# Hybrid SSD and forgetting-attention layer: where kept-back operand blocks get their high parts, and when three pairs of differences are formed

## The chip, the cores and the metric

The kernel runs on one core of one Trainium2 chip. The time is device microseconds of one execution, from launch to end; lower is better. A core has a matmul engine (TensorE, PE in the profile, with the weight loads shown apart as PEld), a vector engine (DVE), a scalar engine (ACT), a general engine (POOL) and a queue that issues most of the transfers (SP). Each engine works through its own queue of instructions in order and waits at the head of it when an instruction's inputs are not there.

## What is computed

One layer with 1024 positions of 1024 channels, in fp32. A projection makes the inputs of two branches: a chunked Mamba-2 scan, and forgetting attention with 16 heads of 64 channels. The two are gated, projected, merged and projected again.

```
h    = RMSNorm_pre(x);  [z_ssm | xBC | dt | q | k | v | f | z_att | g_ssm | g_att] = h @ w_in
A    = chunked SSD scan of silu(conv(xBC)), normed by groups with silu(z_ssm)
s    = q.k / sqrt(64) + F[t] - F[s],  F = cumsum(log sigmoid(f)),  causal
B    = (softmax(s) @ v) * silu(z_att)
m    = sigmoid(g_ssm) * (A @ w_branch_ssm) + sigmoid(g_att) * (B @ w_branch_att)
out  = x + RMSNorm_post(m @ w_out)
```

## The kernel before

**Seven products for eight.** Every large product (the projection, both branch products, the output product) is cut into 2 by 2 blocks and done with seven block products in place of eight. `Pair` holds one pair of weight columns, `Operands` the seven moving operands of one matrix: four blocks b11, b21, b22 and the differences t1 to t4. The three users in the part that matters are `ops_s` (the scan's output), `ops_a` (the attention's output) and `ops_w` (the output weights). To keep fp32 accuracy each operand is two tiles: a high part, a rounded copy that ScalarE makes, and a low part, the raw value less the high part, which VectorE makes. The operands of one name are four tiles of 128 by 512, j = 0 to 3. In the profile they carry the numbers x0 (b11), x1 (b21), x2 (-b22), x3 (t1), x4 (-t2), x5 (t3) and x6 (t4), with h or l behind. A block product takes twelve matmuls: for each j high by high, high by low, low by high.

**The stream.** `Stream.steps` is a written list of block products. `half()` issues half of one (six matmuls), then lets each `Operands` object under way do a little (`some`), then runs one entry of the list `chores`. `some` counts a step, issues the transfers of up to two raw blocks whose source is there (`fetch`, L257), and makes high and low parts (`split`, L265) of up to two blocks that were fetched more than four steps ago. With a name in `only`, it does whatever that name still lacks; `half()` calls it so just before a product that needs the name.

**The attention loop** has 48 turns, m = 6·hp + g: eight pairs of heads hp, six groups g of query and key blocks. A turn issues, in this order: the score matmuls of the turn, with a VectorE operation each that adds the forget terms and finds the row extreme (L1513), and a ScalarE exponential each (L1517), four of both; the value products of the turn before (`weighted`, tile av); the list `deferred`; `stream.release()`; some halves of the stream ("ahead"); the loads; the transposes of the exponentials (tile pt, in the same four PSUM banks as the scores s) with their copies p to SBUF by ScalarE (L1556) or VectorE (L1554); the outputs of an earlier group (`Heads.out`); then `stream.hold()` and one or two halves more ("behind"). The next turn's score matmuls come after these.

Between `hold()` and `release()` no `some` runs at the end of a half: each is put on the list `held` and run at `release()`, behind the next turn's exponentials. So transfers, high parts and low parts of those halves are kept back until then.

**Differences of the late pairs.** When the attention output of pairs hp = 4 to 7 is done for the second half of the positions (`outputs` with h = 1, called from `out(1)` at the end of the turn with g = 5), the blocks t2 and t3 of j = hp - 4 are formed from it, from t1 (tile x) and from b11 (tile y, loaded at L1577 into one of the four buffers of `small`). The function `second` does this with two VectorE operations (L1602, L1603), and two halves later a chore stores both through POOL's queue (L193). For hp = 4, 5 and 6 `second` goes on the list `deferred` and runs in turn 6·(hp + 1), right after that turn's score operations; `last` (L1617), for t4, runs two turns later and first empties the list of chores.

**What sets the order.** A scheduler orders the instructions of each engine and may move one up when it expects its inputs sooner. `pin` queues an instruction behind the one issued just before it on its engine. Score operations and exponentials are pinned, so are high and low parts and the differences; copies of products (L410), weight parts (L350, L351) and the copies p are not.

Of the kernel before, what the change touches and what calls it, by code (L numbers as in the profile page):

```python
# [11 lines left out]
AF = mybir.ActivationFunctionType  # L12
ALU = mybir.AluOpType
# [73 lines left out]
def hybrid_layer(ctx: ExitStack, tc, a, out):  # L87

    nc = tc.nc
# [43 lines left out]
    def pin(op):  # L133
        return tc.keep_in_program_order(op)
# [7 lines left out]
    second = ExitStack()  # L142
# [16 lines left out]
    class Operands:  # L159
# [9 lines left out]
        def __init__(self, name, src, there=lambda k, h: True, order=lambda op: op, queue=nc.gpsimd):  # L169
            self.src, self.there, self.order, self.queue = src, there, order, queue  # L170
            self.copy = src
            self.tiles, self.left, self.made, self.at, self.step = {}, {}, set(), {}, 0
            self.lows, self.most, self.lag = {}, 1, {}
            self.dram = {n: tc.dram_tile([KH, P, HALF], F32, name=f"{n}_{name}") for n in self.LESS}

        def __getitem__(self, name):
# [85 lines left out]
            r, c = self.BLOCKS.get(block, (0, 0))  # L262
            nc.sync.dma_start(raw, self.copy(KH * r + j, c) if block in self.BLOCKS else self.dram[block][j])

        def split(self, name, j, raw=None):  # L265
            h, l = (t[:, j, :] for t in self.tiles[name])
            if name.strip("-") in self.lows:

                pin(nc.scalar.activation(h, h.bitcast(F32), AF.Copy, scale=-1.0 if name[0] == "-" else 1.0))
                self.left[name].remove(j)  # L270
                return
            if raw is None:
                raw = l.bitcast(F32)
            if name[0] == "-":
                pin(nc.scalar.activation(h, raw, AF.Copy, scale=-1.0))
                pin(nc.vector.scalar_tensor_tensor(l, raw, -1.0, h, ALU.mult, ALU.subtract))
            else:
                pin(nc.scalar.activation(h, raw, AF.Copy))
                pin(nc.vector.tensor_tensor(l, raw, h, ALU.subtract))  # L279
            self.left[name].remove(j)  # L280

        def direct(self, j, y, x):

# [7 lines left out]
                self.at[name, j] = self.step  # L291
                self.split(name, j, raw)

        def some(self, only=None):

            self.step += 1
            n = 0
            for name in list(self.left):
                for j in list(self.left[name]):
                    if (only is None and n < 2 or name == only) and (name, j) not in self.at:  # L300
                        if self.ready(name.strip("-"), j):
                            self.fetch(name, j)
                            self.at[name, j] = self.step
                            n += 1
            n, most = 0, self.most if "merged" in fin else 2
            for name, j in list(self.at):
                if j in self.left[name]:
                    if name == only or only is None and n < most and self.at[name, j] < self.step - 4:
                        self.split(name, j)
                        n += 1  # L310

    def column_halves(key):
# [162 lines left out]
    class Stream:  # L475
# [74 lines left out]
        def half(self):  # L550
# [16 lines left out]
            else:  # L567
# [4 lines left out]
                if p in self.following:  # L572
                    ops = self.following[p]
# [5 lines left out]
            for ops in self.building:  # L579
                if self.held is None:  # L580
                    ops.some()
                else:
                    self.held.append(ops)
            for chores in (self.chores, self.line):
                if chores:
                    chore = chores.pop(0)
                    if chore:
                        chore()
# [11 lines left out]

        def release(self):
            held, self.held = self.held or [], None
            for ops in held:
                ops.some()

# [462 lines left out]
    fin = {}  # L1068
# [113 lines left out]
    with tc.tile_pool(name="pro", bufs=1, reuse_waits="tile", side="right") as pro, tc.tile_pool(  # L1182
        name="prop", bufs=1, space=PSUM, reuse_waits="tile", side="right"
# [7 lines left out]
        low = pro.tile([P, NK, HALF], F32, name="low")  # L1191
# [63 lines left out]
        for j in range(KH):  # L1255
# [11 lines left out]
            with tc.high_priority():  # L1267
# [5 lines left out]
                last = put("-t2", j, t2, -1.0)  # L1273
# [24 lines left out]
    with tc.tile_pool(name="ssm", bufs=1, reuse_waits="tile", side="right") as sp, tc.tile_pool(  # L1298
        name="ssmp", bufs=1, space=PSUM, reuse_waits="tile", side="right"
# [38 lines left out]
    with tc.tile_pool(name="att", bufs=1, reuse_waits="tile", side="right") as ap, tc.tile_pool(  # L1338
# [55 lines left out]
        class Heads:  # L1394
# [16 lines left out]
            def settle(self, n):  # L1411

                if n == 2:
                    return
                nr = ap.tile([P, 2, 2], F32, tag="nr", name="nr")
                dd = self.dd[n] = ap.tile([P, 2, 2, 2], F32, tag="dd", name="dd")
                nm = self.nm[n]
                nc.vector.tensor_tensor(nr, nm[:, :, 0], nm[:, :, 1], ALU.min)
                for h in range(2):
                    nc.vector.tensor_tensor(dd[:, :, h], nr, nm[:, :, h], ALU.subtract)  # L1420
                nc.scalar.activation(dd, dd, AF.Exp)
# [148 lines left out]
                    skip_group_check=True,  # L1570
                )

        state, deferred = {}, []

        def fetched(name, j):
            y = small("y")
# [6 lines left out]
        def outputs(hp, h, zr):  # L1583
# [14 lines left out]
            j, x = hp - KH, state["t"]  # L1598
# [21 lines left out]
            if hp == NK - 1:  # L1620
                second()
            else:

                deferred.append(second if h else last)

        def loads(m):

# [75 lines left out]
        for m in range(6 * NK + 1):  # L1703
# [43 lines left out]
            if m == 6 * NK - 1:  # L1747
                tp = pp.tile([P, HALF], F32, tag="s", bufs=4, name="tp")
                heads[hp].turn(2, tp)
                heads[hp].send(2, tp)  # L1750
            stream.hold()
            stream.halves(behind)
            for hd, which in end(m if m == 6 * NK - 1 else m - 1):
# [60 lines left out]
```

## Time and profile before

| what | time |
|---|---|
| median of 3 runs | 1262.39 us |
| lowest and highest of them | 1260.47 and 1264.7 us |
| the profiled execution, its own time | 1261.39 us |
| its span, first to last instruction | 1259.7 us |
| mean granted TensorE clock of the span | 0.997 |
| attention turns, first to last exponential | 677.4 to 1098.2 us |

The profile is of one execution. Busy times of PE are from modelled ends, so a busy PE may still be held up inside a row of matmuls. Times in the views count from the span's start. In a timeline the bracket behind a row is the idle time of that engine before it and what ended that; rows of one kind that follow each other are merged, with their count. Turn 30, which is spoken of below, has its first exponential at 940.0 us, turn 31 at 950.4 us, turn 47 at 1095.9 us.

### The profile page before, as it was taken

Reading aid. Unit: us, or ns where it says so; the run is one execution under the profiler, and the core shown is the slowest. Engines: PE = TensorE matmul, PEld = TensorE weight load, DVE = VectorE, ACT = ScalarE, POOL = GpSimd, SP = SyncE. Lnnn points to the kernel's source line nnn. Section 1 sums busy time; section 2 is a strip of 40 time slices with the busy share of each in tenths; the row PEclk is TensorE's granted clock in tenths of the full one; section 3 lists DMA queues with packets and bytes.
Section 4 is the critical chain, followed back from the end, with each engine's and each line's share of the span. In section 5 each row is a group of like instructions: output and inputs, shape, how many; then the busy total and the mean of one; then the engine's idle time right before and its main releaser. Section 6 shows DMA issues by size and latency. Waiting matters only on the chain.

```text
span 1259.7 us, 20886 instructions
## 1 busy us (share of the span) xinstructions
PE 1232.9 (98%) x6864; PEld 986.7 (78%) x6864; DVE 1014.3 (81%) x1989; ACT 789.7 (63%) x1735; POOL 336.4 (27%) x384
## 2 busy tenths in 40 slices
PE   5999999999999999999999999999999999999997
PEld 3688888888888888888887777777776777788886
DVE  7998896988788878998766677766789768897975
ACT  7745765556655765567555666666786667843753
POOL 4000440004300241115111333333222232357062
PEclk9999999999999999999999999999999999999999
DMA  8243442646446542744465575666787567756932
GB/s 300 71 124 85 143 155 96 203 149 184 126 128 207 174 134 96 240 145 137 141 213 189 175 260 199 222 208 207 262 301 245 195 207 251 260 201 201 367 118 99
DMA packets 162476, 233.57 MB, mean 185 GB/s; under 512 B 15200, under 2 KB 73024, under 8 KB 162368
## 3 DMA queue, kind: packets, MB, share of 16 engines
q1 hardware_dynamic: 140160, 196.08, 48.7%
q10 hardware_dynamic: 16704, 18.06, 4.0%
q0 software_dynamic: 5504, 18.09, 3.7%
q8 instruction: 54, 0.88, 0.3%
q14 instruction: 54, 0.44, 0.1%
HBM read 162.99 MB, written 72.34 MB: 187 GB/s over the span
## 4 chain that ended last, share of the span: by engine, by line
PE 85%; DVE 5%; DMA 4%; ACT 4%; issue 1%; SPq 0%; DVEq 0%; ACTq 0%
PE pb L128 36%; PE pc L128 21%; PE pd L128 7%; PE av L128 5%; PE pt L131 5%; PE s L128 5%; PE yps L128 2%; DMA xt<-in_x 1%; DVE wop L351 1%; PE st L128 1%; DMA y<-ya_dram 1%; PE tr L131 1%; DVE sum L356 1%; PE tr_v L131 1%; ACT wop L350 1%
## 5 line engine op out<-in xcount | busy, mean ns | idle before, releaser
L350 ACT ACTIVATE wop<-sum 128x512 fp32r<-128x512 f32 x180 | 112.2, 625 | 102.4 <-DVE sum L356 49.4
L351 DVE TENSOR_TENSOR wop<-sum,wop 128x512 fp32r<-128x512 f32 x180 | 138.1, 768 | 46.9 <-ACT wop L350 45.6
L1517 ACT ACTIVATE ex<-ex,nm 128x512 f32<-128x512 f32 (+1 forms) x192 | 116.3, 607 | 75.1 <-DVE nm L1513 72.6
L410 ACT ACTIVATE s<-pb 128x512 f32<-128x512 f32 x143 | 84.6, 591 | 88.7 <-PE pb L128 86.4
L128 PE MATMUL pb<-x0h,wop 128*128 128x512 f32 x384 | 132.2, 400 | 0.0
L128 PE MATMUL pc<-x3h,wop 128*128 128x512 f32 x384 | 129.7, 396 | 0.4 <-DVE ot L427 0.4
L128 PE MATMUL pc<-x2h,wop 128*128 128x512 f32 x384 | 130.0, 397 | 0.0
L128 PE MATMUL pb<-x4h,wop 128*128 128x512 f32 x384 | 129.1, 395 | 0.0
L128 PE MATMUL pb<-x6h,wop 128*128 128x512 f32 x376 | 126.7, 395 | 1.3 <-ACT s L410 1.3
L128 PE MATMUL pb<-x5h,wop 128*128 128x512 f32 x376 | 126.7, 395 | 0.0
L351 DVE TENSOR_TENSOR wop<-raw,wop 128x512 fp32r<-128x512 f32 x144 | 107.2, 745 | 18.3 <-ACT wop L350 18.3
L350 ACT ACTIVATE wop<-raw 128x512 fp32r<-128x512 f32 x144 | 89.8, 624 | 19.7 <-PE pd L128 9.1
L1513 DVE CUSTOM_DVE_ANT_0 ex<-s,fb 128x512 f32<-128x512 f32 (+1 forms) x128 | 78.9, 651 | 27.1 <-PE s L128 23.8
L128 PE MATMUL pd<-x1h,wop 128*128 128x512 f32 x288 | 95.8, 392 | 0.0
L128 PEld LDWEIGHTS pc<-x3h,wop 128*128 128x128 f32 x384 | 72.1, 188 | 17.7 <-issue 2.4
L128 PEld LDWEIGHTS pb<-x4h,wop 128*128 128x128 f32 x384 | 72.1, 188 | 17.2 <-issue 2.5
L128 PEld LDWEIGHTS pc<-x2h,wop 128*128 128x128 f32 x384 | 72.1, 188 | 17.1 <-issue 2.0
L128 PEld LDWEIGHTS pb<-x0h,wop 128*128 128x128 f32 x384 | 72.7, 189 | 16.1 <-issue 1.5
L211 POOL TENSOR_TENSOR wd<-wd 128x256 f32<-128x256 f32 x32 | 30.9, 966 | 201.6 <-DMA wd<-in_wo 122.5
L128 PEld LDWEIGHTS pb<-x6h,wop 128*128 128x128 f32 x376 | 70.6, 188 | 17.7 <-ACT s L410 1.7
L128 PEld LDWEIGHTS pb<-x5h,wop 128*128 128x128 f32 x376 | 70.6, 188 | 16.3 <-issue 1.5
L128 PE MATMUL pc<-x3l,wop 128*128 128x512 f32 x192 | 75.1, 391 | 1.4 <-DVE x3l L279 1.4
(311 smaller groups left out, 3022.0 us busy)
## 6 DMA issues: line engine op xcount, KB each, us to landing
raw<-in_wu SPq DMA_DIRECT2D x128, 256.0 KB
csb<-cs_dram SPq DMA_DIRECT2D x32, 256.0 KB
q<-q_dram SPq DMA_DIRECT2D x32, 256.0 KB
k<-k_dram SPq DMA_DIRECT2D x16, 512.0 KB
fb<-f_dram SPq DMA_DIRECT2D x16, 512.0 KB
rb<-st_dram SPq DMA_DIRECT2D x48, 128.0 KB
wd<-in_wo SPq DMA_DIRECT2D x40, 128.0 KB
xt<-in_x SPq DMA_DIRECT2D x8, 512.0 KB
```

The source lines that it names most:

```text
L128: return tc.keep_in_program_order(nc.tensor.matmul(*args, **kw))
L131: return tc.keep_in_program_order(nc.tensor.transpose(out_, in_, idn))
L211: pin(nc.gpsimd.tensor_tensor(t[out_], t[a_], t[b_], ALU.subtract))
L350: nc.scalar.activation(op[:, 0], src, AF.Copy)
L351: nc.vector.tensor_tensor(op[:, 1], src, op[:, 0], ALU.subtract)
L356: self.adds.tensor_tensor(t, x, y, ALU.add)
L410: nc.scalar.activation(s, ps, AF.Copy)
L1513: nc.vector.tensor_tensor_reduce(o, s[e][:, 0:w], f[:, e], 1.0, 3.0e38, ALU.add, ALU.min, nm)
L1517: pin(nc.scalar.activation(o, o, AF.Exp, scale=-1.0, bias=nm, accum_out=hd.at(hd.sm, i, h, e)))
```

## The change

There are two edits.

First, a half that ends while `some` is kept back now also calls `some` with `later`, the number of calls that the object has on the list. Such a call counts no step and fetches nothing. It takes at most one block, the first that the later call at `release()` could have taken, and has ScalarE make its high part at once; the low part is put on a list `owed`. `release()` first has VectorE make the owed low parts (`settle`), then runs the kept-back calls as before. A product that needs a name has that name's owed parts made first.

Second, `second` of hp = 4, 5 and 6 goes on a list of its own, `later`. That list is run in turns with m divisible by six, after the transposes, the copies and `out`, and before `stream.hold()`. `last` stays on `deferred`.

```diff
-        def split(self, name, j, raw=None):
+        def split(self, name, j, raw=None, later=False):
...
-            if name[0] == "-":
-                pin(nc.scalar.activation(h, raw, AF.Copy, scale=-1.0))
-                pin(nc.vector.scalar_tensor_tensor(l, raw, -1.0, h, ALU.mult, ALU.subtract))
+            pin(nc.scalar.activation(h, raw, AF.Copy, scale=-1.0 if name[0] == "-" else 1.0))
+
+            def low():
+                if name[0] == "-":
+                    pin(nc.vector.scalar_tensor_tensor(l, raw, -1.0, h, ALU.mult, ALU.subtract))
+                else:
+                    pin(nc.vector.tensor_tensor(l, raw, h, ALU.subtract))
+
+            if later:
+                self.owed.append((name, low))
             else:
-                pin(nc.scalar.activation(h, raw, AF.Copy))
-                pin(nc.vector.tensor_tensor(l, raw, h, ALU.subtract))
+                low()
             self.left[name].remove(j)
+
+        def settle(self, only=None):
+
+            owed, self.owed = self.owed, []
+            for name, low in owed:
+                if only in (None, name):
+                    low()
+                else:
+                    self.owed.append((name, low))
...
-        def some(self, only=None):
-
-            self.step += 1
+        def some(self, only=None, later=0):
+
+            self.step += not later
+            if only:
+                self.settle(only)
             n = 0
-            for name in list(self.left):
+            for name in [] if later else list(self.left):
...
-            n, most = 0, self.most if "merged" in fin else 2
+            n, most = 0, 1 if later else self.most if "merged" in fin else 2
             for name, j in list(self.at):
                 if j in self.left[name]:
-                    if name == only or only is None and n < most and self.at[name, j] < self.step - 4:
-                        self.split(name, j)
+                    if name == only or only is None and n < most and self.at[name, j] < self.step + later - 4:
+                        self.split(name, j, later=later > 0)
                         n += 1
...
                 else:
                     self.held.append(ops)
+                    ops.some(later=self.held.count(ops))
...
             held, self.held = self.held or [], None
+            for ops in held:
+                ops.settle()
             for ops in held:
                 ops.some()
...
-        state, deferred = {}, []
+        state, deferred, later = {}, [], []
...
-                deferred.append(second if h else last)
+                (later if h else deferred).append(second if h else last)
...
                 heads[hp].send(2, tp)
+            if m % 6 == 0:
+                for fn in later:
+                    fn()
+                later.clear()
             stream.hold()
```

More of the change, by code (lines that the diff above doesn't have):

```diff
@@ L173, in __init__ @@
             self.lows, self.most, self.lag = {}, 1, {}
+            self.owed = []
             self.dram = {n: tc.dram_tile([KH, P, HALF], F32, name=f"{n}_{name}") for n in self.LESS}
```

## The prediction

> **What bounds the kernel now.** I read the page first, then who TensorE waited for, then the clock in short stretches, then the order on each engine where TensorE stood still.
>
> ```profile
> span 1259.7 us, 20886 instructions
> ...
> PE 1232.9 (98%) x6864; PEld 986.7 (78%) x6864; DVE 1014.3 (81%) x1989; ACT 789.7 (63%) x1735; POOL 336.4 (27%) x384
> ...
> PE   5999999999999999999999999999999999999997
> ```
>
> TensorE is busy 98% of the span, and the forty slices show that what is missing lies in the first and the last. The change adds no work and takes none away: the same high parts, low parts and differences are made in another order. So it can only give back time in which TensorE stood still, or add some. The waits of TensorE from 860 us, where the blocks of `ops_s` and `ops_a` are split, to the end of attention, and then those after it (engine, line and releaser; us in total, times, longest):
>
> ```profile
> PE s L128 <- DVE p L1554: 2.1, 1, 2.1
> PE pc L128 <- DVE x3l L279: 1.4, 1, 1.4
> PE s L128 <- ACT p L1556: 0.5, 2, 0.3
> ```
> ```profile
> PE pc L128 <- DVE ot L427: 0.4, 1, 0.4
> ```
>
> These are all, 4.0 us, in four stalls. After attention there are 0.4 us more, so time saved before passes on to the end. A stall can cost more than its length, as short windows around the first one show (busy time of PE, PEld, DVE, ACT and POOL with counts; then granted clock, share of the DMA engines, GB/s); the last row is the stall on x3l:
>
> ```profile
> 945.50:948.90 3.40, 1.37 (x12) 1.05 (x12) 3.40 (x6) 3.40 (x9) 2.95 (x5) 1.00 1.01 369
> 948.90:952.40 3.50, 3.50 (x22) 2.36 (x19) 3.50 (x9) 2.24 (x6) 0.00 (x0) 0.51 0.63 253
> 952.40:960.00 7.60, 7.60 (x51) 6.09 (x52) 6.97 (x16) 3.92 (x9) 1.52 (x3) 1.00 0.60 194
> ...
> 1099.30:1101.30 2.00, 0.62 (x5) 0.29 (x3) 1.43 (x3) 1.94 (x5) 0.00 (x0) 1.00 0.85 296
> ```
>
> Right behind the 2.1 us stall the clock was granted at 0.51 for 3.5 us, and full again after. Work at 0.51 lags by (1 - 0.51) x 3.5 = 1.7 us. Behind the 1.4 us stall it stayed at 1.00. So what the change can reach is 4.0 + 1.7 = **5.7 us**.
>
> **The first stall** is turn 30's. VectorE's order there, the transfer in the chain of waits, ScalarE's copies, and TensorE:
>
> ```profile
> 935.61 8.91 DMA y<-ya_dram
> ...
> 941.48 0.68 DVE L1602 TENSOR_TENSOR x<-zr,x 128x512 f32<-128x512 f32 x1
> 942.07 0.68 DVE L427 TENSOR_TENSOR th<-s,pc 128x512 f32<-128x512 f32 x1
> 944.64 0.69 DVE L1603 TENSOR_TENSOR y<-x,y 128x512 f32<-128x512 f32 x1 [1.89 <-DMA y<-ya_dram]
> 945.25 1.29 DVE L279 TENSOR_TENSOR x3l<-x3l,x3h 128x512 fp32r<-128x512 f32 x2
> 946.46 0.69 DVE L351 TENSOR_TENSOR wop<-sum,wop 128x512 fp32r<-128x512 f32 x1
> 947.06 0.42 DVE L1554 COPY p<-pt 128x256 f32<-128x256 f32 x1
> ...
> 945.45 1.10 ACT L1556 ACTIVATE p<-pt 128x256 f32<-128x256 f32 x3
> ...
> 943.69 0.38 PE L131 MATMUL pt<-ident,ex 128*128 128x128 f32 x2
> ...
> 945.08 0.39 PE L128 MATMUL pb<-x4h,wop 128*128 128x512 f32 x1
> 947.53 1.77 PE L128 MATMUL s<-k,q 64*128 64x512 f32 x12 [2.06 <-DVE p L1554]
> ```
>
> The second operation of `second` (L1603) stands at the head of VectorE's queue until its b11 block lands, 1.89 us. Two low parts, a weight part and then the copy p queue up behind it. The copy's input was there at 944.07 (the last transposes, 943.69 + 0.38); it ran at 947.06. The scores of the next turn need that PSUM bank, and TensorE has nothing else in its queue.
>
> **What the second edit does.** It puts L1602 and L1603 behind the copies p. Ahead of this copy go 0.68 + 0.69 us of work and 1.89 us of waiting, 3.26 us with the rows as they overlap; the block has landed by 944.52 (935.61 + 8.91), so the wait itself is gone, not moved. The copy could then end some 3 us sooner, near 944.4, a us before TensorE is ready at 945.47 (945.08 + 0.39). What is late next are ScalarE's three copies: they begin at 945.45, and at 1.10/3 = 0.37 us each the two banks that the first scores need are free by 946.2. Left as they are, they keep up to 0.7 us of the stall; at best nothing is left. The first edit takes one high part from in front of them (below), some 0.5 us, so I keep **0.3 us** and count 2.06 - 0.3 = **1.76 us**.
>
> The 1.7 us of the clock I count in full: the two windows meet at the stall, and the stall left, 0.3 us, is far under the 1.4 us that did no harm at 1099 us. From below this term is nothing.
>
> [...]
>
> The same two operations run for three more pairs (L1602 and L1603: durations min/median/max, then L1603's idle time by what ended it):
>
> ```profile
> L1602 DVE TENSOR_TENSOR x<-zr,x x4: 679/681/683, 941.5 to 1102.6; 128x512 f32<-128x512 f32 x4
> ...
> L1603 DVE TENSOR_TENSOR y<-x,y x4: 683/694/695, 944.6 to 1103.8; 128x512 f32<-128x512 f32 x4
> ...
>   DMA y<-ya_dram: 1.9, 1
> ```
>
> The fourth is the last pair's and isn't moved. Turns 36 and 42 had no wait there, so nothing is gained in them. What the move costs is 0.68 + 0.69 = 1.37 us of VectorE work that now stands between the copies and the next turn's score operations, in three turns. It is hidden where ScalarE's exponentials wait on nothing worse than now, and TensorE has the value products and the halves ahead to do meanwhile. Without that cover it is at most 3 x 1.37 = 4.1 us; I take **0**, since the list of TensorE's waits above has none for an exponential. The chores with the two stores move past masks on POOL's queue by about a turn; nothing needs t2 before the last pair's is made.
>
> **What the first edit does.** By the step rule (fetched more than four steps ago, one block for each kept-back call) I count thirteen high parts that go ahead of exponentials: two each in turns 26 and 28, one each in 29, 30 and 32 for `ops_s`; two each in 44 and 46, one each in 45 and 47 for `ops_a`. What they cost and what room there is (the median of 12 such high parts; ScalarE's waits in 890 to 1100 us; the exponentials of turns 32, 46 and 47):
>
> ```profile
> L278 ACT ACTIVATE x3h<-x3l x12: 610/614/621, 936.2 to 1183.3; 128x512 fp32r<-128x512 f32 x12
> ...
> ACT ex L1517 <- DVE nm L1513: 39.3, 29, 3.9
> ...
> 961.54 0.62 ACT L1517 ACTIVATE ex<-ex,nm 128x384 f32<-128x384 f32 x1 [3.88 <-DVE nm L1513]
> ...
> 1086.71 0.72 ACT L1517 ACTIVATE ex<-ex,nm 128x512 f32<-128x512 f32 x1 [2.53 <-DVE nm L1513]
> ...
> 1095.87 0.62 ACT L1517 ACTIVATE ex<-ex,nm 128x384 f32<-128x384 f32 x1 [0.80 <-DVE nm L1513]
> ```
>
> Thirteen at 0.61 us are 8.0 us of ScalarE, put into 39.3 us in which it stood waiting ahead of exponentials. I count **0** for the cost: turn 46 has 2.53 us of room for 1.2, turn 47 has 0.80 for 0.6. Where a turn has no room, one part delays the exponentials by 0.6 us at most.
>
> Its gain is the second stall. The product with x3 (t1 of `ops_a`) needs all four low parts, and two of them were kept back:
>
> ```profile
> 1098.29 1.13 ACT L278 ACTIVATE x3h<-x3l 128x512 fp32r<-128x512 f32 x2
> ...
> 1099.87 0.69 DVE L1484 TENSOR_TENSOR o<-o,rb 128x512 f32<-128x512 f32 x1 [1.04 <-DMA rb<-st_dram]
> 1100.48 0.68 DVE L279 TENSOR_TENSOR x3l<-x3l,x3h 128x512 fp32r<-128x512 f32 x1
> ...
> 1101.22 0.50 PE L128 MATMUL pc<-x3l,wop 128*128 128x512 f32 x1 [1.38 <-DVE x3l L279]
> ```
>
> Both high parts came after the exponentials, both low parts behind L1484, which itself waited for a transfer. Afterwards one of the two has its high part ahead of 1095.87 and its low part right behind the score operations: j = 0 is in time. The other keeps its high part behind the exponentials, and its low part may still queue behind L1484, to end at 1101.16, when TensorE wants it some three matmuls later than the first. So between 0 and about 0.9 us stay; I take the middle, 0.5, and a gain of 1.38 - 0.5 = **0.9 us**. The 0.5 us of waits for ScalarE's copies I leave as they are.
>
> **The sum:** 1.76 + 1.7 + 0.9 = 4.4 us. The profiled execution took 1261.39 us, so it becomes 1257.0; the median of the runs is 1.0 us above that execution, which gives **1258.0 us**. A change of 0.3% is 3.8 us, about what a measurement of this kernel can tell from none, so the forecast stands hardly beyond that bound.
>
> **The rivals.**
>
> *The stall is handed on.* ScalarE's copies, or 1.37 us more ahead of the next score operations, keep 1 to 2 us of TensorE idle in turn 30 or 31, and the clock may fall again. For it: VectorE is busy all through 948.9 to 952.4 and 81% of the span. Against it: without the wait of 1.89 us VectorE is ahead there. Of the 4.4 us some 1.5 to 2.5 are left: near 1260.4.
>
> *The clock falls in any case.* Then 1.7 us go from the sum, and 1262.39 - 2.7 = 1259.7. Against it: it fell right at the stall and nowhere else in attention. [...]
>
> *No effect.* The scheduler may order the unpinned weight parts and copies anew, so that waits of this size come up elsewhere, as they do by chance now: 1262 give or take 1.
>
> *Slower: the four buffers of `small`.* Tile y is now held from its load to a store a turn later, in turns 30, 36 and 42. The gates, the products' results and the tiles rb share the other three, and SP's queue stops at the first load that finds none:
>
> ```profile
> t_a<-y POOLq DMA_DIRECT2D x4, 256.0 KB, 5.7
> ...
> SPq L1453 <- DMA st_dram<-ex: 42.3, 13, 6.5
> ...
> SPq L1076 <- DVE th L1088: 2.6, 2, 1.9
> ```
>
> SP stands still up to 6.5 us at a time now and TensorE does not notice. If the store's 5.7 us come on top of such a wait, the next queries and rb are late, VectorE stops at L1484 or L1478 as it did for y, and each of the three turns has a stall like turn 30's, 2.06 + 1.7 = 3.8 us. Three are 11.3 us against a gain of 4.4: 1269. It decides from 1.5 us a turn upward. Against it: at the end of turn 30 I find one of the four free again when the next result asks.
>
> **How the numbers follow.** Forecast 0.58; handed on 0.14; clock falls anyway 0.08; no effect 0.12; slower 0.08. The forecast's own range is 1256.0 to 1259.6: the full 5.7 us of the stalls give 1256.7, with 0.7 for the scatter of the median, and the weak end leaves 0.7 us of the first stall, 0.9 of the second and half of the clock's 1.7. The range of 8 in 10 leaves out the slower case and the upper part of no effect: 1256.0 to 1262.6. Faster by over 0.3% means below 1258.6: most of the forecast, 0.45, and 0.02 from the others, 0.47 in all. Slower by over 0.3% means above 1266.2: 0.06. Within: 0.47.
>
> **What would show it.** Right: no wait of PE s for DVE p in turn 31's scores, L1603 without a wait, PEclk 1.00 through 940 to 960 us, x3h once ahead of turn 47's exponentials, and less than 0.9 us of wait for x3l. Wrong: a granted clock near 0.5 anywhere from 860 to 1125 us, waits of PE s or pt for ACT over 1 us, L1603 waiting still, or SP waiting at L1076 with L1484 or L1478 late behind it.

## The result, and the profile after

The changed kernel takes 1260.78 us (median of 22 runs, 1258.48 to 1263.53), the kernel before 1263.05 us (median of 22 runs measured beside them). The ratio is 0.9978, with a 95% interval of 0.9969 to 0.9987. So 0.22%, 2.8 us by the ratio, is gained, and not the 4.4 us of the forecast. Two later comparisons of the same two kernels, described below, gave 0.9976 and 0.9987.

First the head of the profile's page of the changed kernel (span, then busy time and count of each engine):

```profile
span 1261.8 us, 20886 instructions
...
PE 1234.1 (98%) x6864; PEld 987.5 (78%) x6864; DVE 1013.3 (80%) x1989; ACT 789.6 (63%) x1735; POOL 340.4 (27%) x384
```

The instructions are the same 20886, and the engines' busy times differ by little. This execution took 1263.53 us, the longest of its 22, so its span can't be set against that of before. What can be compared is who TensorE waited for (engine, line and releaser; total, times, longest, in us). Lines of the changed kernel stand some 20 further down: L1554 is now L1575, L1556 is L1577, L1602 and L1603 are L1623 and L1624, L279 is L281, L1432 is L1453.

```profile
PE tr_v L131 <- DVE th L441: 1.6, 1, 1.6
...
PE s L128 <- DVE p L1575: 1.4, 1, 1.4
PE av L128 <- ACT p L1577: 1.0, 1, 1.0
```

The 2.1 us wait of turn 30 and the 1.4 us wait for x3l are gone. A 1.4 us wait of scores for a copy p by VectorE is there, but it is another one: that of turn 32's scores, a turn later. The 1.0 us wait of value products for ScalarE's copies is new, too. The wait for tr_v ends at 180.07 us, long before anything that the change touches.

TensorE's 6864 matmuls come in the same order in both traces. So I take the start of each in one trace less its start in the other, and look where that difference changes. The table gives the changes between points of before's time, in us; negative is gained. Before's own trace has its 3.5 us at a clock of 0.51, a lag of 1.7 us, in the first stretch. All traces of this study stand in it, to be used below.

| kernel | 945-953 | 953-963 | 963-1095 | 1095-1103.5 | 1103.5-1106 | 1106-1250 | sum, 860-1250 |
|---|---|---|---|---|---|---|---|
| after | -3.59 | +2.12 | -1.75 | -1.70 | +1.10 | +1.20 | -2.63 |
| after again (e4) | -3.33 | +3.87 | -1.72 | -1.46 | +0.03 | +1.36 | -1.20 |
| after again (e10) | -3.60 | +2.08 | -1.66 | -1.35 | 0.00 | +0.75 | -3.77 |
| second edit alone (e1) | -3.20 | +1.53 | +1.04 | +0.90 | +0.91 | +0.02 | +1.21 |
| first edit alone (e2) | +3.32 | 0.00 | -1.73 | -1.70 | +0.93 | +2.15 | +3.30 |
| before, y early (e3) | -2.59 | 0.00 | +0.08 | +0.02 | -0.01 | +0.01 | -2.45 |
| first edit, y early (e5) | -2.47 | +0.01 | -1.20 | -1.39 | 0.00 | +0.91 | -4.13 |
| after, copy on ScalarE (e6) | -3.59 | +0.49 | -0.37 | -1.33 | 0.00 | +0.27 | -4.47 |
| after, budget (e7) | -2.73 | +1.50 | -0.48 | -1.39 | 0.00 | +1.24 | -1.83 |
| first edit, y early, budget (e8) | -3.36 | +0.41 | -1.16 | -1.35 | 0.00 | +1.32 | -4.12 |
| before, copy on ScalarE (e9) | +0.99 | -0.27 | +0.27 | +0.06 | 0.00 | +0.29 | +1.37 |
| after, copy on ScalarE, budget (e11) | -3.55 | +0.46 | -0.84 | -1.38 | -0.01 | +0.98 | -4.30 |

Row by row it shows the same: turn 30 gives what was forecast, the stall on x3l more than was forecast, and between 953 and 963 us and after 1104 us a good part is given back. Up to 860 us, where nothing was changed, all twelve traces lie 1.8 to 4.8 us behind before's: the execution whose profile the forecast started from was a quick one.

**Turn 30 and what follows it.** VectorE in the changed kernel (start, duration, engine, line, operation, output and inputs, shape; a bracket would be idle time before it):

```profile
950.27 0.42 DVE L1575 COPY p<-pt 128x256 f32<-128x256 f32 x1
950.60 0.68 DVE L1623 TENSOR_TENSOR x<-zr,x 128x512 f32<-128x512 f32 x1
951.32 0.80 DVE L1624 TENSOR_TENSOR y<-x,y 128x512 f32<-128x512 f32 x1
...
958.55 0.68 DVE L1109 SCALAR_TENSOR_TENSOR th<-th 128x512 f32<-128x512 f32 x1
959.16 0.68 DVE L369 TENSOR_TENSOR wop<-raw,wop 128x512 fp32r<-128x512 f32 x1
959.76 1.67 DVE L1453 TENSOR_TENSOR sm<-sm,dd 128x8 f32<-128x8 f32 x1
961.35 0.68 DVE L1575 COPY p<-pt 128x512 f32<-128x512 f32 x1
```

The two operations of the pair now follow the copy and wait for nothing. But 9 us later L1453, on 128 by 8 elements, takes 1.67 us, and the copy p of turn 31 stands behind it. What TensorE does at these two places, and at the later ones:

```profile
950.15 1.75 PE L128 MATMUL s<-k,q 64*128 64x512 f32 x12
...
962.08 0.61 PE L128 MATMUL s<-k,q 64*128 64x256 f32 x5 [1.42 <-DVE p L1575]
...
1101.41 0.39 PE L128 MATMUL pc<-x3l,wop 128*128 128x512 f32 x1
...
1105.07 1.36 PE L128 MATMUL av<-p,v 128*64 128x256 f32 x12 [0.98 <-ACT p L1577]
```

The scores of turn 31 (950.15) wait for nothing any more; those of turn 32 stand still for 1.42 us in their midst, until the copy behind L1453 has run. How long L1453 usually takes, in the changed kernel and, as L1432, in before (minimum, median, maximum in ns):

```profile
L1453 DVE TENSOR_TENSOR sm<-sm,dd x16: 160/168/1667, 691.0 to 1082.1; 128x8 f32<-128x8 f32 x16
```
```profile
L1432 DVE TENSOR_TENSOR sm<-sm,dd x16: 159/167/169, 686.2 to 1079.8; 128x8 f32<-128x8 f32 x16
```

Only one of sixteen is long, and only after the change. Beside it POOL works on the masks; its rows of the changed kernel:

```profile
959.53 0.54 POOL L1110 DMA_DIRECT2D ms_dram<-th  x1 [6.57 <-DVE th L1109]
960.09 1.30 POOL L1409 TENSOR_TENSOR ex<-fb,far 128x256 f32<-128x256 f32 x2
```

The two mask operations run from 960.09 to 961.39, and L1453 ends at 961.43. In before the same pair of masks was there, at 959.04, but VectorE came to it in another order:

```profile
956.80 0.16 DVE L1432 TENSOR_TENSOR sm<-sm,dd 128x8 f32<-128x8 f32 x1
...
958.08 0.68 DVE L1554 COPY p<-pt 128x512 f32<-128x512 f32 x1
958.68 2.22 DVE L1478 TENSOR_TENSOR zr<-o,rb 128x512 f32<-128x512 f32 x1
```

There the copy was ahead, and L1478 was the operation drawn out beside the masks: 2.22 us, where the median of its eight in before is 0.685. Nobody on TensorE needed it soon. In the changed kernel the scheduler has put the 128 by 8 product between the store's operation (L1109) and the copy. The masks follow that store on POOL (959.53, then 960.09), so VectorE gets to L1453 0.33 us before they begin. What the rows show is this: L1453 took 1.67 us against a median of 0.168 and ended 0.04 us behind the masks (961.43 against 961.39); before's L1478 took 2.22 us against its 0.685 and ended 0.56 us behind them (960.90 against 960.34). L1453 begins 0.33 us before POOL's masks and L1478 0.36 us before them, and both are drawn out. That the masks hold them is read from these times; in what way they do isn't shown.

**The end of attention.** VectorE, then ScalarE, in the changed kernel:

```profile
1098.37 1.89 DVE L281 TENSOR_TENSOR x3l<-x3l,x3h 128x512 fp32r<-128x512 f32 x3
...
1100.30 0.63 DVE L281 TENSOR_TENSOR x3l<-x3l,x3h 128x512 fp32r<-128x512 f32 x1
...
1102.76 0.69 DVE L1505 TENSOR_TENSOR o<-o,rb 128x512 f32<-128x512 f32 x1 [1.75 <-DMA rb<-st_dram]
```
```profile
1095.67 1.13 ACT L275 ACTIVATE x3h<-x3l 128x512 fp32r<-128x512 f32 x2
...
1102.38 0.60 ACT L439 ACTIVATE th<-pb 128x512 f32<-128x512 f32 x1 [2.62 <-issue]
1102.87 0.62 ACT L368 ACTIVATE wop<-raw 128x512 fp32r<-128x512 f32 x1
1103.39 1.14 ACT L275 ACTIVATE x2h<-x2l 128x512 fp32r<-128x512 f32 x2
1104.43 1.34 ACT L1577 ACTIVATE p<-pt 128x512 f32<-128x512 f32 x3
```

Three of the four high parts of x3 are made ahead of turn 47's exponentials, one more than before; the fourth follows them at 1099.14 us. All four low parts run ahead of L1505 (L1484 before), which still waits for rb. So nothing of the x3l stall is left. The 1.10 us lost right after it, however, come from L439 (L421 before), which stood 2.62 us at the head of ScalarE's queue, with a weight part, two high parts and the three copies p behind it. The profile names no releaser here; the first edit alone, below, shows one.

### The profile page after: what moved, and what is told of

Same layout as the page of the kernel before. It is cut to its first block, busy times and chain, and to the rows that moved or that the text cites. A ratio compares the mean times of both kernels' runs of the same rounds, so it can differ in the third digit from the quotient of the medians.

```text
span 1261.8 us, 20886 instructions
## 1 busy us (share of the span) xinstructions
PE 1234.1 (98%) x6864; PEld 987.5 (78%) x6864; DVE 1013.3 (80%) x1989; ACT 789.6 (63%) x1735; POOL 340.4 (27%) x384
## 4 chain that ended last, share of the span: by engine, by line
PE 81%; DVE 6%; DMA 5%; ACT 5%; issue 2%; SPq 1%; POOL 0%; DVEq 0%; ACTq 0%; POOLq 0%
PE pb L128 35%; PE pc L128 20%; PE pd L128 6%; PE pt L131 5%; PE av L128 5%; PE s L128 4%; PE yps L128 2%; DMA xt<-in_x 1%; DVE wop L369 1%; PE st L128 1%; ACT ex L1538 1%; DVE sum L374 1%; PE tr L131 1%; PE tr_v L131 1%; ACT wop L368 1%
## 5 line engine op out<-in xcount | busy, mean ns | idle before, releaser
L128 PE MATMUL pb<-x0l,wop 128*128 128x512 f32 x192 | 75.7, 394 | 0.0
```

The source lines that it names most:

```text
L128: return tc.keep_in_program_order(nc.tensor.matmul(*args, **kw))
```

## The experiments

The theory after the comparison: turn 30's stall came from waiting for the b11 block alone, and the second edit cures it; what it gives back is the copy p behind a drawn-out VectorE operation a turn later; the first edit cures x3l and loses a little later on. The rivals: the gain is the clock's and not the stall's; the loss at turn 32 is chance; the losses after 1104 us come from releases that now make more blocks than before.

### e1: the second edit alone

```diff
-        state, deferred = {}, []
+        state, deferred, later = {}, [], []
...
-                deferred.append(second if h else last)
+                (later if h else deferred).append(second if h else last)
...
+            if m % 6 == 0:
+                for fn in later:
+                    fn()
+                later.clear()
```

> The second edit alone. Theory: it takes away turn 30's stall of 2.1 us and the half-speed clock behind it (1.7 us), and hands on 1.4 to 1.8 us, because its 1.37 us of VectorE work now pushes the copy p of turn 31 behind a vector operation that POOL's masks stretch; the stall on x3l near 1100 us (1.4 us) stays. So 1.5 to 2.5 us under the kernel before, and in the trace a wait of PE s for DVE p in turn 32's scores. Rival (the handed-on wait comes from the first edit's order of VectorE): no such wait, and 3.5 to 4 us under.

Measured: 1263.12 us against 1264.55 of before, ratio 0.9987 (0.9977 to 0.9997). TensorE's waits in its profile:

```profile
PE pc L128 <- DVE x3l L279: 1.7, 1, 1.7
PE s L128 <- ACT p L1556: 1.6, 2, 1.4
PE s L128 <- DVE p L1554: 0.4, 1, 0.4
```

Turn 30 gains 3.20 us; the stall on x3l stays, as it must. The 1.4 us wait of turn 32's scores for VectorE's copy, which was expected, did not come: the copy p of turn 31 is hardly late, and the scores wait 0.4 us. With this edit alone the scheduler leaves the copy ahead of the drawn-out operation. VectorE there:

```profile
958.28 0.68 DVE L1554 COPY p<-pt 128x512 f32<-128x512 f32 x1
958.88 2.12 DVE L1478 TENSOR_TENSOR zr<-o,rb 128x512 f32<-128x512 f32 x1
```

Still 1.53 us are handed on between 953 and 963 us, 0.85 of it at the transposes of turn 31, whose exponentials come later behind the 1.37 us of moved work. The 1.4 us wait for ScalarE's copies is that of turn 47's scores, at 1093.81 us, 0.25 us in before; it makes the +1.04 of the table. The clock also fell, to 0.50, behind the 1.7 us stall on x3l in this execution (1104.2 to 1107.6). So the runs show 1.6 us of the 3.2 that the edit's own stretch gains.

### e2: the first edit alone

```diff
-                (later if h else deferred).append(second if h else last)
+                deferred.append(second if h else last)
```

> The first edit alone. Theory: it takes away the stall on x3l (1.4 us) and nothing else, since the wait for tile y is still at the head of VectorE's queue in turn 30; the stall there is 1.5 to 2.1 us with the low clock in most executions. 0.5 to 1.5 us under the kernel before. Rival (the wait for y does harm only because the low parts and copies behind it are late anyway, so that high parts made sooner hide it): turn 30's stall under 0.5 us, and 3 us or more under.

Measured: 1264.46 us against 1264.55, ratio 0.9994 (0.9981 to 1.0007): no gain that can be told. TensorE's wait, VectorE's wait for the block, the clock behind it (window, its length, busy times and counts of the five engines, granted clock, DMA share, GB/s), and ScalarE near the end:

```profile
PE s L128 <- DVE p L1575: 3.2, 2, 2.5
```
```profile
947.91 0.69 DVE L1624 TENSOR_TENSOR y<-x,y 128x512 f32<-128x512 f32 x1 [3.37 <-DMA y<-ya_dram]
```
```profile
951.40:958.20 6.80, 5.50 (x25) 3.76 (x26) 6.49 (x18) 4.07 (x10) 0.35 (x1) 0.50 0.76 261
```
```profile
1104.39 0.60 ACT L439 ACTIVATE th<-pb 128x512 f32<-128x512 f32 x1 [2.44 <-DMA ms_dram<-th]
```

The stall of turn 30 is there in full, and the clock at 0.50 for 6.80 us, where before had 3.5 us at 0.51. The x3l stall is gone (-1.70). The same L439 stands here for 2.44 us, and its releaser is the landing of a store of a gated product: L439's tile is one of the four buffers of `small`, and the one that comes free next is held by that store. This time is lost in two of the nine traces with the first edit (after and e2); in the other seven that stretch of the table loses nothing. (The 0.91 us of e1 in that stretch are the clock's.)

### e3: before, with the b11 block loaded a turn earlier

```diff
-            if g == (5 if more else 4) and hp >= KH:
+            if g == 4 and hp >= KH:
                 state["y"] = fetched("b11", hp - KH)
```

> The kernel before, with the b11 block of tile y loaded one turn sooner (at g = 4 in place of 5 for hp from 4) and nothing moved on VectorE. Theory (the late transfer is what costs, not the place of the two vector operations): L1603 waits for nothing, turn 30 has at most 0.3 us of stall and a full clock, nothing is handed on to turn 31: 3 to 4 us under the kernel before, more than with the second edit. Rival (the place of the operations matters): turn 30 still loses 0.7 us or more for the copies, under 2 us gained. Second rival (the four buffers of small): tile y takes one a turn longer, and SP's queue waits at L1076 or L1453: no gain or a loss.

Measured: 1263.0 us against 1264.55, ratio 0.9989 (0.998 to 0.9998). VectorE keeps before's order, but L1603 waits for nothing:

```profile
945.24 0.69 DVE L1603 TENSOR_TENSOR y<-x,y 128x512 f32<-128x512 f32 x1
...
947.65 0.42 DVE L1554 COPY p<-pt 128x256 f32<-128x256 f32 x1
```

This is the cleanest line of the table: -2.59 us in turn 30, nothing elsewhere. The mean granted clock of this execution was 0.999, against 0.997 in the trace of before. But the stall isn't gone whole. TensorE at turn 31's scores:

```profile
948.13 2.30 PE L128 MATMUL s<-k,q 64*128 64x512 f32 x12 [0.38 <-DVE p L1554]
```

They still wait 0.38 us for the copy p, which stands behind the same low parts and weight part as in before, and the row of twelve takes 2.30 us, against 1.75 in the changed kernel, while ScalarE's copies p run until 949.41 us. So most of the stall was the transfer's, but not all: the place of the work has some 0.9 us in it (0.38, and 2.30 less 1.75). The 3 to 4 us that were expected did not come; the ratio gives 1.4 us. That is as much as the second edit alone gives (0.9987), which gains more in turn 30 (3.20) and hands some of it on.

### e4 and e10: the changed kernel again

> The changed kernel once more, for its scatter and a second profile. Theory: the wait of PE s for DVE p in turn 31 to 32 (1.4 us) and the absence of the waits in turn 30 and on x3l come again, since they follow from the order of the queues; the stall near 178 us with the low clock behind it, and ScalarE's 2.6 us of idleness near 1100 us that the profile puts down to nothing, do not, since nothing was changed there. 2 to 3 us under the kernel before in the median. Rival (those two belong to the changed program): both come again.

> The changed kernel, unaltered, beside the other two of this call, so that they can be compared on one chip. Near 0.9976 of before, as in the two times that it was measured; a wait of turn 32's scores for DVE p of about 1.4 us again if that wait belongs to the order of the work and not to chance.

Measured: 0.9976 (0.9963 to 0.9989) and 0.9987 (0.9974 to 1.0). In both, as in the first profile, scores of turn 32 wait 1.4 us for DVE p, and L1453 takes 1.66 or 1.67 us: three of three, so it is no chance. Of the other two stalls of the first profile, the 2.62 us of L439 came in neither, the wait for tr_v in e10 alone. What differs at turn 32 is the clock behind it: in e4 it fell to 0.50, in the other two it was 1.00. The window of e4:

```profile
960.70:964.10 3.40, 3.40 (x17) 1.71 (x14) 1.87 (x12) 2.81 (x9) 0.51 (x1) 0.50 0.76 180
```

and the same stretch of e10, then of the first profile of the changed kernel, with the window ahead of which before had its drop:

```profile
960.70:964.20 3.50, 3.17 (x24) 2.13 (x25) 3.44 (x16) 1.98 (x7) 0.56 (x1) 1.00 0.42 109
```
```profile
949.00:952.40 3.40, 3.40 (x24) 2.40 (x24) 3.37 (x7) 3.23 (x9) 2.52 (x4) 1.00 0.95 299
...
960.70:964.20 3.50, 2.12 (x21) 1.48 (x21) 3.50 (x12) 0.93 (x3) 1.25 (x3) 1.00 0.64 211
```

Half of the 3.40 us at 0.50 is 1.7 us; that drop is why e4 loses 3.87 us where the others lose 2.1.

### e5: the first edit with the early load

```diff
-                (later if h else deferred).append(second if h else last)
+                deferred.append(second if h else last)
...
-            if g == (5 if more else 4) and hp >= KH:
+            if g == 4 and hp >= KH:
```

> The first edit with tile y loaded one turn sooner, in place of the second edit. Theory (the second edit's cure and the wait that it hands on are apart: the cure is the transfer's, the wait comes from 1.37 us of VectorE work put ahead of turn 31's score operations): no wait of PE s for DVE p at turn 32's scores, no wait on x3l, and 2.5 to 3.5 us under the kernel before, at least as good as both edits (3.0 us in the median). Rival (the order of VectorE that the first edit brings makes the wait in turn 32 by itself): that wait of 1.4 us comes again, and under 2 us gained.

Measured: 1260.73 us (9 runs) against 1265.32, ratio 0.9966 (0.995 to 0.9983). No score waits for DVE p. VectorE in turn 31:

```profile
957.48 0.16 DVE L1453 TENSOR_TENSOR sm<-sm,dd 128x8 f32<-128x8 f32 x1
957.56 0.68 DVE L1109 SCALAR_TENSOR_TENSOR th<-th 128x512 f32<-128x512 f32 x1
...
958.76 0.68 DVE L1575 COPY p<-pt 128x512 f32<-128x512 f32 x1
959.36 1.62 DVE L1499 TENSOR_TENSOR zr<-o,rb 128x512 f32<-128x512 f32 x1
```

The order is before's: the short product first, the copy ahead of the masks, and L1499 (L1478 before) is the one drawn out. The first edit by itself does not bring about the bad order, nor does the second (e1); in these builds it takes both.

### e6: both edits, and turn 31's copy on ScalarE

```diff
-                    if b % 4 == 1 and hp < NK - 2:
+                    if b % 4 == 1 and hp < NK - 2 and g != 1:
```

> The changed kernel with the one copy p of the turns with g = 1 that VectorE made given to ScalarE (eight copies of 0.37 us). Theory (in turn 31 that copy is queued on VectorE behind the small product of row sums, which a pair of POOL's mask operations stretches from 0.17 to 1.67 us): the stall of 1.4 to 1.6 us at turn 32's scores goes, with the low clock that follows it in some executions: 1 to 2 us under the changed kernel, 4 us under the kernel before. Rival (TensorE would wait for the next copy anyway, since ScalarE has four in a row now): a wait of PE s for ACT p of 0.7 us or more in turn 32 or in other turns with g = 1, and no gain.

Measured: 1259.65 us (6 runs) against 1265.32, ratio 0.9962 (0.995 to 0.9974). VectorE and TensorE in turn 31 and 32:

```profile
957.12 1.67 DVE L1453 TENSOR_TENSOR sm<-sm,dd 128x8 f32<-128x8 f32 x1
```
```profile
957.07 1.41 PE L128 MATMUL s<-k,q 64*128 64x384 f32 x12
```

The product is drawn out as in the changed kernel, to the same 1.67 us, but no copy stands behind it, and turn 32's scores wait for nothing. This is the direct proof of the cause: the operation's length does no harm without the copy in its queue.

### e7 and e8: fewer blocks at the release

A release makes one block less for each that was made ahead; e8 has it on top of e5.

```diff
-            self.owed = []
+            self.owed, self.spent = [], 0
...
-            n, most = 0, 1 if later else self.most if "merged" in fin else 2
+            n, self.spent = (min(1, self.spent), max(self.spent - 1, 0)) if only is None and not later else (0, self.spent)
+            most = 1 if later else self.most if "merged" in fin else 2
...
+                ops.spent += len(ops.owed)
                 ops.settle()
```

> The changed kernel, where a kept-back call that finds an owed low part makes one block less, so that a release makes no more low parts in a row than before the change. Theory (owed low parts on top of two blocks a call put x5l later than TensorE wants it, 0.4 us near 1110 us, and shift later ones, 0.3 and 0.6 us near 1119 and 1190): those three losses go, 0.5 to 1.3 us under the changed kernel. Rival (they come from the order that the scheduler finds, whatever the count): they stay, within 0.4 us of the changed kernel.

> The first edit with the smaller release and the early load of tile y. Theory: it adds up, 3 to 4.5 us under the kernel before and 0.5 us or more under both edits. Rival (what is saved after 1105 us is taken by a later wait): the same as the kernel with the early load and the first edit.

Measured: e7 1261.01 us, 0.9972 (0.9963 to 0.9981); e8 (5 runs) 1259.73 us, 0.9963 (0.9951 to 0.9976), both against 1265.32. The loss after 1106 us is not smaller with it (+1.24 and +1.32), and the wait of turn 32 is there in e7 (+1.50) and not in e8. Nearly all of that loss now lies near 1190 us (1.24 and 1.19), where the six traces with the first edit and the full release have 0.26 to 0.90. So the number of blocks at a release isn't what costs there; for this place the rival falls. The smaller losses between 1106 and 1187 us (0.7 in after and e4, 1.4 in e2) are gone in e7, e8 and e11, but they are gone in e5, e6 and e10 too, which make no block less; for them it stays open. e8 and e5 can't be told apart.

### e9: before, with only turn 31's copy on ScalarE

The diff of e6, without the change.

> The kernel before with nothing of the change: only the one VectorE copy p of the turns with g = 1 goes to ScalarE, as in the run in which both edits had it so. If that copy was worth something only because the second edit had put more work ahead of it, this alone gives nothing: the 2.1 us wait of turn 30's scores for DVE p and the wait of 1.4 us for x3l stay, and the ratio to before is 1.000 give or take 0.001. If the copy's engine was a gain of its own, which the run with both edits merely added to theirs, the ratio is near 0.999 (1.6 us of 1265) and a stall of before in turn 31 or 32 must be gone, though none is listed there.

Measured: 1266.67 us against 1264.16, ratio 1.002 (1.0007 to 1.0032): slower by 0.2%, which neither side had expected. VectorE:

```profile
949.86 0.69 DVE L1603 TENSOR_TENSOR y<-x,y 128x512 f32<-128x512 f32 x1 [2.88 <-DMA y<-ya_dram]
```

The wait of turn 30 for the block has grown from 1.89 to 2.88 us. Its load was issued at 941.01 in this trace; with the 4.24 us by which the trace lies behind there, that is 1.2 us later against the matmuls than in before (935.61), and the scores' wait grew by the same 1.2 us, to 3.3. The mean granted clock of the 12 runs is 0.9968, against 0.9983 in the runs of before beside them, so the longer stall goes with a lower clock as well. Why SP came to the load later I have not followed up. For the question it suffices: the copy's place is no gain of its own, and e6's gain is that of the two edits with their loss removed.

### e11: both edits, the copy on ScalarE and the budget

> Both edits, with the copy of the turns with g = 1 on ScalarE and with the high parts made ahead counted against what the released calls may make. Each alone gave 0.9962 and 0.9972 of before. If the losses of 0.3 to 0.5 us after 1105 us come from the additional blocks that a release makes, both add up and the ratio is near 0.996 or a little below (0.4 to 1 us under the run with the copy alone); if they are chance, it is the same as that run, 0.9962, within 0.001. No wait of PE s for DVE p over 0.5 us by either theory.

Measured: 1259.78 us (12 runs) beside e10's 1261.39 on the same chip and 1264.16 of before, ratio 0.9967 (0.9956 to 0.9978). No score waits for DVE p. It is e6 within the intervals: the budget adds nothing (+0.98 after 1106 us). Against before, e5, e6, e8 and e11 thus lie at 0.9962 to 0.9967, the changed kernel at 0.9976 to 0.9987. Only e11 was measured beside the changed kernel, 1.6 us under it in the median. Of the four, e5 and e6 need the least: one number in place of the second edit, or one more condition.

## Why the prediction was right and wrong

**Right: what the wait was.** Turn 30's stall came for the most part from the b11 block, and most of it goes with the wait for it: in e3, with nothing moved, 2.06 us of wait become 0.38. What e3 leaves is the place of the work, ScalarE's copies among it, which the forecast had named as what is late next. The three traces of the changed kernel gain 3.3 to 3.6 us there, where the forecast counted 1.76 of the stall and 1.7 of the clock, 3.46. The signs that were named came: no wait of turn 31's scores, L1603 without a wait, a clock of 1.00 to 960 us, one more high part of x3 ahead of turn 47's exponentials. One of the signs of the contrary came as well: in e4 the clock fell to 0.50 at 960.7 us, within the 860 to 1125 us that were named.

**Wrong in size: "The 1.7 us of the clock I count in full".** In the trace of before it is so, but the clocks of before's runs lie between 0.996 and 1.000, so they don't all have it, and the changed kernel has drops of its own (to 0.50 in e4 at 960.7 us, to 0.51 at 180.7 us in its first profile). Over 82 runs of before in the later comparisons the mean granted clock was 0.9982, over 46 runs of the changed kernel 0.9984. That is 0.0002 of 1260 us, about 0.3 us instead of 1.7. (The clocks are listed with three decimals, so this is a rough figure.) By this estimate some 1.4 us go off the sum. Where the profile has a longer stall, the mean clock of the runs is lower: with 2.5 us the 12 runs of e2 have 0.9971, with 3.3 us those of e9 0.9968, against before's 0.9982 with 2.06 us.

**Wrong: the cost of the moved 1.37 us, taken as 0.** The forecast's reason was that no exponential is waited for. Between 953 and 963 us 2.1 us were lost (3.9 with a drop). Some 0.4 of it, at 955.8 us, is the direct delay of turn 31's exponentials. The larger part, 1.6, is the order: with both edits the copy p stands behind a product that took 1.67 us in place of 0.17 beside the masks on POOL. The rival "the stall is handed on" had the place and the size of this (1 to 2 us, clock perhaps again), but not the mechanism; e6 shows the latter. What made the scheduler choose that order isn't shown.

**Not foreseen: 963 to 1095 us.** There the nine traces with the first edit gain 0.4 to 1.8 us, the three without it lose 0.1 to 1.0. The forecast counted no gain in these turns, and left ScalarE's copies (0.5 us of waits) as they were. The largest gains lie at the scores of turns 33 and 47. Those of turn 33, in before and in the changed kernel:

```profile
966.79 2.15 PE L128 MATMUL s<-k,q 64*128 64x512 f32 x12
```
```profile
970.09 1.66 PE L128 MATMUL s<-k,q 64*128 64x512 f32 x12
```

The row is 0.5 us shorter without a wait in the list for it: before's TensorE is held up within the row, where ScalarE makes two high parts x2 between the exponentials and its copies p (963.74, 1.14 us), and the changed kernel one (965.46, 0.62). The first edit alone has the short row as well (1.66), the second alone has not (2.02). All nine traces with the first edit gain 0.5 us there. So this gain is the first edit's, and a sum drawn up from the list of waits, as the 5.7 us of the forecast were, can't see it. At turn 47 the traces with the first edit lie between 0.8 us gained and 0.5 lost, and what decides that isn't shown.

**Wrong, the other way: x3l.** Counted 0.9, with 0.5 left; the traces of the changed kernel gain 1.35 to 1.70 and nothing is left, since the last low part, which the forecast left behind L1484, comes ahead of it.

**Wrong: the first edit's cost, taken as 0.** After 1106 us the nine traces with it lose 0.27 to 2.15 us, on average 1.1; the three without it lose 0.01 to 0.29. The step that failed was looking for its cost only in the turns in which high parts are moved. Some 0.8 us of it, on average over the nine, are at one place, here in e10's trace:

```profile
1189.75 0.50 PE L128 MATMUL pb<-x5h,wop 128*128 128x512 f32 x1 [0.45 <-ACT s L428]
```

A product there waits for a copy s that ScalarE makes; before had no wait at it. It isn't the number of blocks at a release (e7, e8, e11); why these copies are later stays open. The 1.0 us at 1104 us in after and e2 is, by the releaser that e2 shows, a shortage of `small` buffers, as the slower rival had feared, but by another holder: it had named tile y, a load that SP can't issue, and 3.8 us a turn. A fifth buffer wasn't tried.

**In sum**, over the three traces of the changed kernel the stretches come to -3.5, +2.7, -1.7, -1.5, +0.4 and +1.1 us, -2.5 in all, against the forecast's -4.4. The runs show -2.3 by the medians and -2.8 by the first ratio. That the traces agree with them so well is in part luck, since before's one trace has a full drop of the clock in it, and of the changed kernel's three only one. The measured 1260.78 lies above the forecast's own range, 1256.0 to 1259.6, within the wider one, to 1262.6, and nearest to the time of "the stall is handed on", 1260.4, which was given 0.14. And 0.7 us of the predicted 1258.0 was the base: the median of before that it started from was 1262.39, beside the changed kernel it is 1263.05.

## What to carry to other kernels

When a wait at the head of a queue is the stall, first load earlier (one number, e3): here it gained about as much of the whole time as moving the work behind the wait, 0.9989 against 0.9987, and moved nothing that can be late elsewhere. When work is reordered, look again at which small operation each PSUM copy now stands behind, and what the neighbouring engine runs at that moment; a row that takes ten times its median is the sign (here 1.67 us against 0.168, beside POOL's masks). A matmul row that is longer than others of its kind can hide a wait that no list shows (here turn 33's scores, 2.15 us against 1.66). A term of the clock read from one execution should be counted by how often it occurs, and not in full (here 1.7 us were counted, and the mean clocks give about 0.3).

## What the runs showed of the hardware that was not expected

Behind the start and ahead of the end, the granted clock falls in these traces to 0.50 for 3.41 us, in e2 for twice that (951.40 to 958.20 us). In before its changes at 20.50, 948.93 and 952.34 us lie 272 times and once 3.41 us apart, in the first profile of the changed kernel those at 23.70, 180.72 and 184.13 us 46 times and once. Which stall it falls behind isn't decided by the stall's length alone. Counted in stretches of 3.41 us laid off from such a change, by the modelled ends, TensorE stood idle for 1.97 us or more in three, and the clock fell at the end of all three (before with 2.01 us; e2 and e9, whose waits there are 2.5 and 3.3 us). Of eight stretches with 1.42 to 1.74 us it fell at the end of three (after at 180.7, idle for 1.74 of the 3.40 us ahead of it; e1 and e4, behind waits of 1.7 and 1.4 us) and not of the other five (e5, e9 and e10 near 180, with waits of 1.6 us; after and e7 near 963, with waits of 1.4). Behind stretches with less it did not fall (the most is 1.37 us in before and 1.31 in after); in e2 the stretch right behind the fall still has 1.26 us of idleness, and the clock stayed at half for one more. The same place of the same kernel, in the first profile and in e10's, which keeps the same stall of 1.63 us there:

```profile
180.70:184.20 3.50, 3.50 (x10) 2.70 (x9) 3.03 (x7) 2.93 (x8) 0.87 (x2) 0.51 0.49 120
```
```profile
180.70:184.20 3.50, 3.50 (x17) 2.90 (x16) 2.33 (x5) 3.36 (x10) 1.36 (x2) 1.00 0.47 135
```

So a stall of 1.63 us had a clock of 0.51 behind it in one trace and of 1.00 in the other, and in e4 a wait of 1.4 us came ahead of a fall. What decides between them isn't shown.

The other is the VectorE product on 128 by 8 elements that took 1.66 or 1.67 us instead of 0.17 beside two mask operations on POOL, in all six traces of kernels with both edits (after, e4, e10, e6, e7, e11), whichever engine made the copy; in the traces with one edit or none it never took more than 0.17 us.
